# One-pass logits with doubled queries and keys, an earlier memory attention, filler at four rates, and a regrouped opening and output projection in a two-layer encoder trunk

## The chip, the cores and the metric

The kernel runs on one core of one Trainium2 chip. The metric is the device time of one execution in microseconds (us). Three runs of the kernel before gave 1203.88, 1205.63 and 1206.22; their median, 1205.63, is the time before.

## The reference, cut to what matters

The trunk has two layers on 512 tokens of width 1024 in fp32. Each layer normalises the tokens, projects them, mixes them over the sequence, attends beside that to 256 memory tokens in four heads, projects the concatenated result, adds it to the residual, and then runs a gated MLP with a causal convolution. Layer 0 mixes by differential attention in six heads of two 64-wide halves; layer 1 mixes by chunked gated linear attention (GLA).

```python
# layer 0, per head h, half m (0, 1), query block of 128 tokens
q = rms_norm(q, qk_norm_g[0]) * (d ** -0.5)          # d = 64
k = rms_norm(k, qk_norm_g[1])
logits = einsum('bhmqd,bhmkd->bhmqk', q, k) + bias   # keys up to the query's chunk
p = softmax(logits)
w = p[:, :, 0] - lam * p[:, :, 1]
o = rms_norm(w @ v, out_norm_g) * (1.0 - lam_init)
# both layers
x = x + concat([mix, cross]) @ w_out[i]
x = x + conv_ffn(rms_norm(x, ffn_norm[i]))
```

## The kernel before, in words

**Precision and weights.** Large products are made from float32r operands in one pass each. An operand is split into a hi part (a cast) and a lo part (what the cast lost), and three matmuls, hi·hi, hi·lo and lo·hi, stand for one fp32 matmul: gemm (L250 to L252) for projections whose output has tokens on the partitions, product (L267 to L269) for those whose output is transposed. The moving side is up to 512 columns wide. Weights come in pieces: SP loads a raw tile, ACT casts hi (L200), DVE subtracts lo (L201); activations are split by ACT (L233) and DVE (L234). Small products, the attention's logits (L613), values (L649) and all transposes (L169), are plain fp32 matmuls; the profile shows an fp32 matmul that is no transpose as two records.

**Order.** The order on PE is the order of the text. On the other engines a scheduler orders the instructions. Between steps of the attention PE gets filler: a queue of units of large products (class Filler, L89) from which `fill(us)` takes as many as its argument pays for, by costs written in the code. `need` runs the queue up to a mark, `flush` runs all of it.

**Memory of the matmuls.** There are four tags of PSUM banks with two banks each: mm for large products, sm for values and some large products, lg for logits, tp for transposes.

**Layer 0's attention** (diff_layer, L554) is a loop of 28 steps t (L681). Step t does logits(t), values(t - 2), a fill, turn(t - 1), a slot of memory attention, and a fill again; a step index u is head u // 4, query block i = u % 4, and the logits of block i have 128·(i + 1) keys. prepare(h) (L581) transposes the four token blocks of a head's normalised q and of its k into a tp bank each, and ACT copies them out (L589). The two 64-wide halves of a head then lie on partitions 0 to 63 and 64 to 127, and logits (L613) multiplies each half by itself, in 64-row matmuls, into its own lg bank; from the second block on each is cut in two. DVE adds the bias and takes the maximum (L618), ACT takes the exponentials (L621), DVE joins the halves. turn (L631) transposes the weights, values (L641) multiplies them by v, finish(h) (L658) transposes the head's output and splits it. Heads 0 and 1 are prepared before the loop, the others at t = 7, 8, 15, 16; their norms (group_norm, L299: squares on ACT L303, sums L304 and the scaling L307 on DVE) are at t = 5, 6, 13, 14. Memory attention (MemAttn, L473) starts its slots at t = M0 = 12, with its norm at t = 8, the memory keys' transposes (keys0) at t = 9 and its queries (L487) at t = 11. Each step fills twice 3.0 us up to t = 13 and 1.2 us from there.

**The output projection** (out_proj) goes in parts given by PASS, a list per layer of output column groups c with the mix tiles ks that they take; mix tiles 0 to 5 are the heads and 6, 7 the memory attention. A part's tiles are filler; the last part of each layer comes behind the loop. A finished tile is added to the residual on DVE (update, L969), split for the MLP (L233, L234), and its squares are summed (L335). The MLP starts with row_scales (L1026), which needs the squares of all tiles.

**The opening** (L354 to L420) loads, on SP, the columns of norm gains (cols_a), then the x tiles and weight blocks in turn, and multiplies the first projection as they arrive, in an order written by hand on all engines (operands(k), matmuls L420); ACT's queue loads the first weights. Its four banks are then evicted with r_x, the tokens' norm factors.

**GLA** makes its gates (L799 to L807) for four heads, each a small matmul (L800) into an lg bank, then ACT (absolute value, exponential, logarithm: L802 to L804) and DVE (L805, a scan L807).

Of the kernel before, what the change touches and what calls it, by code (L numbers as in the profile page):

```python
# [10 lines left out]
F32 = mybir.dt.float32  # L11
F32R = mybir.dt.float32r
# [19 lines left out]
WB = 5  # L32
FA, FB = 3.0, 1.2
K8 = tuple(range(KT))
# [3 lines left out]
         [(2, (6, 7, 4, 5)), (0, (4, 5)), (3, (6, 7, 4, 5)), (1, (4, 5))]],  # L38
        [[(c, (0, 1, 2, 6, 7)) for c in C4], [(c, (3, 4, 5)) for c in C4]])

# [87 lines left out]
@with_exitstack  # L128
def trunk(ctx, tc, x_t, mem_t, wpack, cols_a_d, cols_d, conv_d, gate_d, rel_bias, diff_lambda, consts, onehot, out):
    nc = tc.nc  # L130
# [167 lines left out]

    def group_norm(pool, y, nb, ng, d, on_dve=False):  # L299
        ss = small("ss")  # L300
        for b in range(0, nb, 2):
            sq = xtile()[:, :2 * ng * d]
            A.activation(sq, y[:, b:b + 2].rearrange("p b n -> p (b n)"), AF.Square)  # L303
            V.reduce_sum(ss[:, b * ng:(b + 2) * ng], sq.rearrange("p (g d) -> p g d", d=d), axis=AX.X)  # L304
        r = rsqrt(ss[:, :nb * ng], nb * ng, 1.0 / d, on_dve)
        yv = y.rearrange("p b (g d) -> p (b g) d", d=d)
        V.tensor_mul(yv, yv, r.unsqueeze(2).to_broadcast([128, nb * ng, d]))  # L307

# [35 lines left out]
    def small_vectors():  # L344
        for c in (c_dq, c_mq(0), c_mq(1)):
            V.tensor_scalar_mul(c, c, 0.125)
        V.tensor_scalar_mul(c_do, c_do, 1.0 - LAM_INIT)
        for t in range(3):
            V.tensor_scalar_mul(c_go(t), c_go(t), 0.5)
        lam(lv, xtile()[:, 0:128].rearrange("p (a b) -> p a b", a=2))  # L350
# [3 lines left out]
    with tc.tile_pool(name="ini", bufs=1) as ip, tc.manual_schedule(engines={E.Activation, E.DVE, E.Pool, E.SP}):  # L354
# [12 lines left out]
        A.dma_start(raws[0][:, blk(0, S)], wpack[0, :, blk(0, S)])  # L367
        load(cols_a, cols_a_d)
        for k in range(KT):
            xT[k] = xtile()  # L370
            load(xT[k], x_t[k])
            if k:
                load(raws[k // 2][:, blk(k % 2, S)], wpack[k // 2, :, blk(k % 2, S)])
        at[0] = 4
# [9 lines left out]
        def operands(k):  # L384
            if k % 2 == 0:
                split_w[0] = [wp.tile([128, WTILE], F32R, name=n, tag=n, bufs=WB) for n in ("whi", "wlo")]
            c = blk(k % 2, S)
            hi, lo = split_w[0]
            xh[k], xl[k] = split_tiles()
            if k == 0:  # L390
                V.tensor_copy(hi[:, c], raws[0][:, c])
                V.tensor_sub(lo[:, c], raws[0][:, c], hi[:, c].bitcast(F32))
                split(xh[0], xl[0], xT[0], c_attn(0, 0))
            else:
                split(xh[k], xl[k], xT[k], c_attn(0, k))
                split_weights(c, raws[k // 2], hi, lo)
            parts.append((hi[:, c], lo[:, c]))
            squares(xT[k], acc)
# [41 lines left out]
    def mem_kv(l):  # L440
# [18 lines left out]
        def keys():  # L459
            F.need(f"kv{l}")  # L460
            p = bank("lg")
            for hp in range(2):
# [4 lines left out]
             (lambda: token_rsqrt("lg", mem_acc[0], 2, r_mem)) if l == 0 else None)  # L467
        F.add(0.0, lambda: group_norm(None, km[0], 2, 4, 64))
        F.mark(f"kv{l}")
# [3 lines left out]
    class MemAttn:  # L473
# [4 lines left out]
        def norm(self):  # L478
            group_norm(self.pool, self.qm, NB, 4, 64, self.on_dve)

# [72 lines left out]

    def diff_layer(pool, mix):  # L554
        r = r_x[:, 0]
# [7 lines left out]
        def halves(d0, d1):  # L563
# [3 lines left out]
            return ev  # L567

        def project_qk(pr):
            qk[pr] = (pool.tile([128, NB, 256], F32, name="qs", bufs=1),  # L570
                      pool.tile([128, NB, 256], F32, name="ks", bufs=1))
            gemm(xh, xl, NB, ("qk", pr), 512, halves(*qk[pr]))
            F.mark(f"qk{pr}")

        heads = {}

        def norms(pr, i):
            F.need(f"qk{pr}")
            group_norm(pool, qk[pr][i], NB, 4, 64)

        def prepare(h):  # L581
            pr, j = divmod(h, 2)
            t2 = []
            for src, g, nm in zip(qk[pr], (c_dq, c_dk), ("qT", "kT")):
                dst = pool.tile([128, S], F32, name=nm, bufs=3)
                p = bank("tp")
                for b in range(NB):
                    transpose(p[:, blk(b)], src[:, b, blk(j)])
                A.activation(dst, p, AF.Copy, scale=g)  # L589
                t2.append(dst)  # L590
            sm = cp.tile([128, 16], F32, name="smd", tag="smd")
            heads[h] = dict(q=t2[0], k=t2[1], s2=sm.rearrange("p (m b) -> p m b", b=8),
                            nm=small("nmd"), rc=small("rcd"), v=vs[pr], j=j)

        live = {}

        def logits(u):
# [10 lines left out]
            pls = bank("lg"), bank("lg")  # L608
            cuts = (0, nk) if i == 0 else (0, nk // 2, nk)
            for k0, k1 in zip(cuts, cuts[1:]):  # L610
                for m in range(2):
                    hh = blk(m, 64)
                    mm(pls[m][:, k0:k1], H["q"][hh, blk(i)], H["k"][hh, k0:k1], start=True, stop=True)  # L613
            for m in range(2):
# [26 lines left out]
        def values(u):  # L641
            h, i = divmod(u, 4)
            H = heads[h]
            if i == 0:
                F.need(f"v{h // 2}")
                H["po"] = bank("sm")
            po, wT = H["po"], live.pop(u)
            for kb in range(i + 1):
                mm(po[:, blk(i)], wT[:, blk(kb)], H["v"][:, kb, blk(H["j"])], start=kb == 0, stop=kb == i)  # L649
            if i == 3:  # L650
                rs = small("rs0")
                V.reciprocal(rs[:, :NB], H["s2"][:, 0, :NB])
                o = H["o"] = pool.tile([128, NB, 128], F32, name="o", bufs=2)
                V.tensor_mul(o, po.rearrange("p (b d) -> p b d", d=128),
                             rs[:, :NB].unsqueeze(2).to_broadcast([128, NB, 128]))
                group_norm(pool, o, NB, 1, 128)

        def finish(h):  # L658
            p = bank("tp")
            for b in range(NB):  # L660
# [4 lines left out]

        qk[0] = (pool.tile([128, NB, 256], F32, name="qs", bufs=1),
                 pool.tile([128, NB, 256], F32, name="ks", bufs=1))
        ev = halves(*qk[0])
        for b in range(NB):
# [4 lines left out]
        F.mark("v0")  # L674
        F.fill(10.0)
        prepare(0)
        F.fill(1.2)
        prepare(1)
        ma = MemAttn(pool, 0, qm, mix, False)
        M0 = 12  # L680
        for t in range(28):  # L681
            if t == 0:
# [6 lines left out]
                ops1, keys1 = mem_kv(1)  # L689
            if t == 8:  # L690
                ma.norm()
            if t == 9:
                keys0()
# [9 lines left out]
            if t in (20, 24):  # L703
                out_proj(0, mix, t // 4 - 4, None)
            f = FA if t < 14 else FB
            if t == 11:
                ma.queries()
# [5 lines left out]
            if t in (5, 6, 13, 14):  # L713
                norms((t + 3) // 8, (t + 3) % 8)
            if 0 <= t - 1 < 24:
                turn(t - 1)
            ma.slot(t - M0)
            F.fill(f)
            if t in (7, 8, 15, 16):
                prepare(2 * (t // 7) + (t + 1) % 8)  # L720
            if t % 4 == 3 and t >= 7:
                finish(t // 4 - 1)
        F.flush()


    def gla_layer(pool, mix, acc):
# [71 lines left out]
        for h in range(4):  # L798
            pz = bank("lg")  # L799
            mm(pz[:96], gw3[:, blk(h, 96)], gl3, start=True, stop=True)  # L800
# [133 lines left out]
        for h in range(4):  # L934
# [15 lines left out]
            outputs(h, 1)  # L950
            group_norm(pool, o_[h], NB, 1, 192, True)
            F.fill(f)
# [29 lines left out]

    def out_proj(l, mix, part, acc):
        got = {}
        turns = cycle(("mm", "sm") if part == len(PASS[l]) - 1 else ("mm",))

        def unit(c, ks, n, i):
            if i == 0:
                if c not in got:
                    got[c] = weights(("o", l, part, c))  # L990
                got["p"] = bank(next(turns))
            p = got["p"]
            product(p, got[c], n, [mix[k] for k in ks], (i,))
            if i == len(ks) - 1:
                update(2 * c + n, p, None if acc is None else (lambda k: c_ffn(l, k)), acc, G if l else V)
        todo, kk = tiles(l, part)
        for n in todo:
            for i in range(len(kk[n // 2])):
                F.add(0.65, lambda n=n, i=i: unit(n // 2, kk[n // 2], n % 2, i))

# [71 lines left out]
    for l in range(2):  # L1072
        with tc.tile_pool(name=f"at{l}", bufs=2) as pool:
            mix = [None] * 8
            if l == 0:
                diff_layer(pool, mix)
            else:
                gla_layer(pool, mix, acc)
            acc = [None]
            out_proj(l, mix, len(PASS[l]) - 1, acc)  # L1080
            F.flush()
        with tc.tile_pool(name=f"ff{l}", bufs=2) as pool:
# [74 lines left out]
```

## Time and profile before

| | us |
|---|---|
| median of three runs | 1205.63 |
| profiled execution | 1205.31 |
| its span | 1203.5 |
| PE busy | 1188.3 (99%) |
| DVE busy | 759.8 (63%) |
| ACT busy | 540.7 (45%) |
| POOL busy | 23.5 (2%) |

All times of the trace are from one profiled execution; it took 1205.31 us, of which 1203.5 are the span from the first instruction to the last. The costliest groups of PE are the one-pass matmuls of 512 columns, L267 to L269 in mm banks alone 460 of each line. The chip's DMA queues moved 117.80 MB, most of it weights, at a mean of 98 GB/s. Stages that the text speaks of, by the trace's clock: the opening up to about 31 us, the loop of layer 0's attention from the first logits at 45.35 to the last at 227.78, its end up to L1026 at 269.30, GLA's gates around 650, the end of layer 1's mixer at 842.64.

In the views of the trace a line gives start, duration, engine, line of the code, operation, result <- operands, the shape, and, in brackets, how long the engine was idle before it and what released it. "x8" joins eight neighbours of one kind.

### The profile page before, as it was taken

To read this page: it belongs to the slowest core of one execution; us is meant where nothing else is said; L and a number is where in the kernel's file an instruction comes from. 1 tells how busy PE (TensorE), PEld (TensorE's weight loads), DVE (VectorE), ACT (ScalarE), POOL (GpSimd) and SP (SyncE) were. 2 spreads that over 40 slices of the span, in tenths; PEclk is the share of its full clock that TensorE was granted. 3 is DMA by queue.
4 is the path that set the end of the run, shared out by engine and by line. 5 is a ranking of instruction groups with operands and counts; after the bars stand their busy time and mean duration, and the time that the engine had idled before them with its cause. 6 is when DMAs were issued, how large, how long until landed. Compare 5 with 4: busy or idle time off the path is not lost.

```text
span 1203.5 us, 14757 instructions
## 1 busy us (share of the span) xinstructions
PE 1188.3 (99%) x5672; PEld 975.0 (81%) x5672; DVE 759.8 (63%) x1259; ACT 540.7 (45%) x915; POOL 23.5 (2%) x37
## 2 busy tenths in 40 slices
PE   9999999999999999999999999999999999999998
PEld 6887777778888888888787888987888888888887
DVE  7566578887776534767546446768677653476741
ACT  6666666554444222434436444536444432243420
POOL 0000000000000000000020000003000000000000
PEclk9999999999999999999999999999999999999999
DMA  8432231232332331422342221234233233232231
GB/s 275 132 101 84 80 118 49 71 105 88 98 112 70 123 105 53 130 80 88 116 146 74 70 71 57 62 127 133 78 98 112 71 123 97 67 122 84 87 114 44
DMA packets 39413, 117.80 MB, mean 98 GB/s; under 512 B 4688, under 2 KB 5769, under 8 KB 39343
## 3 DMA queue, kind: packets, MB, share of 16 engines
q1 hardware_dynamic: 39198, 116.60, 30.5%
q8 instruction: 44, 0.72, 0.2%
q10 hardware_dynamic: 144, 0.26, 0.1%
q14 instruction: 27, 0.21, 0.1%
HBM read 112.63 MB, written 4.21 MB: 97 GB/s over the span
## 4 chain that ended last, share of the span: by engine, by line
PE 90%; DVE 5%; ACT 3%; issue 1%; DMA 1%; SPq 0%; DVEq 0%; ACTq 0%
PE ps_mm L268 8%; PE ps_mm L269 8%; PE ps_mm L267 8%; PE ps_sm L267 6%; PE ps_sm L268 6%; PE ps_sm L269 6%; PE ps_mm L250 6%; PE ps_mm L252 6%; PE ps_mm L251 5%; PE ps_tp L267 3%; PE ps_tp L268 3%; PE ps_tp L269 3%; PE ps_lg L268 3%; PE ps_lg L269 3%; PE ps_lg L267 3%; PE ps_tp L169 2%
## 5 line engine op out<-in xcount | busy, mean ns | idle before, releaser
L200 ACT CAST whi<-raw 128x1024 fp32r<-128x1024 f32 (+2 forms) x214 | 207.7, 976 | 247.5 <-PE ps_tp L268 133.8
L201 DVE TENSOR_TENSOR wlo<-raw,whi 128x1024 fp32r<-128x1024 f32 (+2 forms) x214 | 240.8, 1136 | 111.0 <-ACT whi L200 109.9
L267 PE MATMUL ps_mm<-xsh,whi 128*128 128x512 f32 x460 | 182.5, 397 | 0.2 <-DVE xt L969 0.2
L268 PE MATMUL ps_mm<-xsl,whi 128*128 128x512 f32 x460 | 179.4, 390 | 1.4 <-DVE xsl L234 1.3
L269 PE MATMUL ps_mm<-xsh,wlo 128*128 128x512 f32 x460 | 179.3, 390 | 0.0
L268 PE MATMUL ps_sm<-xsl,whi 128*128 128x512 f32 x372 | 144.7, 389 | 0.0
L267 PE MATMUL ps_sm<-xsh,whi 128*128 128x512 f32 x372 | 144.7, 389 | 0.0
L269 PE MATMUL ps_sm<-xsh,wlo 128*128 128x512 f32 x372 | 144.7, 389 | 0.0
L250 PE MATMUL ps_mm<-whi,xsh 128*128 128x512 f32 (+2 forms) x352 | 138.2, 393 | 0.1
L252 PE MATMUL ps_mm<-whi,xsl 128*128 128x512 f32 (+2 forms) x352 | 131.4, 373 | 0.3 <-DVE xsl L234 0.3
L251 PE MATMUL ps_mm<-wlo,xsh 128*128 128x512 f32 (+2 forms) x352 | 130.6, 371 | 0.0
L1019 ACT ACTIVATE cvo<-u,cv 128x512 f32<-128x512 f32 x88 | 71.6, 815 | 114.0 <-DVE u L1017 113.6
L268 PEld LDWEIGHTS ps_mm<-xsl,whi 128*128 128x128 f32 x460 | 86.5, 188 | 20.2 <-DVE xsl L234 2.7
L267 PEld LDWEIGHTS ps_mm<-xsh,whi 128*128 128x128 f32 x460 | 86.4, 188 | 18.2 <-DVE xt L969 0.9
L269 PEld LDWEIGHTS ps_mm<-xsh,wlo 128*128 128x128 f32 x460 | 86.3, 188 | 18.1
L1020 DVE SCALAR_TENSOR_TENSOR cvo<-u,cv,cvo 128x512 f32<-128x512 f32 x88 | 65.9, 749 | 31.6 <-ACT cvo L1019 31.4
L268 PEld LDWEIGHTS ps_sm<-xsl,whi 128*128 128x128 f32 x372 | 69.8, 188 | 14.6
L269 PEld LDWEIGHTS ps_sm<-xsh,wlo 128*128 128x128 f32 x372 | 69.8, 188 | 14.5
L267 PEld LDWEIGHTS ps_sm<-xsh,whi 128*128 128x128 f32 x372 | 69.8, 188 | 14.4
L252 PEld LDWEIGHTS ps_mm<-whi,xsl 128*128 128x128 f32 x352 | 66.1, 188 | 12.7 <-DVE xsl L234 0.5
L250 PEld LDWEIGHTS ps_mm<-whi,xsh 128*128 128x128 f32 x352 | 66.3, 188 | 10.7 <-issue 0.9
L251 PEld LDWEIGHTS ps_mm<-wlo,xsh 128*128 128x128 f32 x352 | 66.5, 189 | 9.5
(247 smaller groups left out, 1767.9 us busy)
## 6 DMA issues: line engine op xcount, KB each, us to landing
raw<-in_wpack_dram SPq DMA_DIRECT2D x176, 512.0 KB, 3.5
raw<-in_wpack_dram SPq DMA_DIRECT2D x27, 256.0 KB, 3.5
xt<-in_x_t_dram SPq DMA_DIRECT2D x16, 256.0 KB, 5.3
xres<-xt SPq DMA_DIRECT2D x8, 256.0 KB, 3.5
xt<-xres SPq DMA_DIRECT2D x8, 256.0 KB, 4.4
out_dram<-xt SPq DMA_DIRECT2D x8, 256.0 KB, 2.0
bt<-bias_d SPq DMA_DIRECT2D x6, 256.0 KB, 5.2
raw<-in_wpack_dram SPq DMA_DIRECT2D x4, 384.0 KB, 2.9
```

The source lines that it names most:

```text
L169: nc.tensor.transpose(dst, src, ident[:n, :n])
L200: A.copy(hi[:, c], raw[:, c])
L201: V.tensor_sub(lo[:, c], raw[:, c], hi[:, c].bitcast(F32))
L250: mm(p, sh[k][:, blk(b)], hi, start=k == 0, stop=False)
L251: mm(p, sh[k][:, blk(b)], lo, start=False, stop=False)
L252: mm(p, sl[k][:, blk(b)], hi, start=False, stop=k == KT - 1)
L267: mm(p, hi[:, blk(n)], bh, start=i == first, stop=False)
L268: mm(p, hi[:, blk(n)], bl, start=False, stop=False)
L269: mm(p, lo[:, blk(n)], bh, start=False, stop=i == last)
L1019: A.activation(c, u[:, 2:], AF.Identity, scale=cv[l][:, 2, j:j + 1], bias=cv[l][:, 3, j:j + 1])
L1020: V.scalar_tensor_tensor(c, u[:, 1:S + 1], cv[l][:, 1, j:j + 1], c, op0=ALU.mult, op1=ALU.add)
```

## The change

1. q and k of a head pair lie in tiles of twice the width, [128, 4 blocks, 4 halves, 2, 64]. For q, slot 1 gets hi (ACT copy to float32r) and slot 0 the rest (DVE); for k the second slot is a copy (ACT). prepare takes one half m of a head: four transposes of a q half, four of a k half, an ACT copy of q (now hi and lo stacked on 128 rows), a split of k (ACT and DVE). Logits are, per half, two one-pass matmuls on 128 rows, with k's hi and lo, over all keys at once. The gains of q and k are joined in the k columns.
2. Memory attention moves from M0 = 12 to 8, its norm to t = 5, keys0 and the queries to t = 7.
3. The fills are 3.2 us (t < 8), 2.1 (t < 13), 1.5 (t < 20) and 1.3, instead of 3.0 (t < 14) and 1.2; ahead of the loop 12.5 instead of 10.0, and 1.2 behind each of four half prepares.
4. In the steps with a prepare, its first half comes behind the first fill, ahead of turn, and the second behind the second fill.
5. Of layer 0's last part of the output projection, four units (twelve matmuls) that do not take head 5 are queued at t = 26 and flushed ahead of finish(5); the rest comes behind the loop. Banks of last parts go mm, mm, sm, sm instead of mm, sm.
6. In the opening the gain columns and x tile 0 are one tensor, loaded first in two parts, and split in two halves; the separate load of cols_a goes behind the last weights.
7. The matmuls of GLA's gates use lg and sm banks in turn.
8. In layer 1, column group 3 takes mix tiles 6 and 7 in the last part instead of the first.

```diff
-FA, FB = 3.0, 1.2
+STEPS, FILL = (8, 13, 20), (3.2, 2.1, 1.5, 1.3)
...
-        [[(c, (0, 1, 2, 6, 7)) for c in C4], [(c, (3, 4, 5)) for c in C4]])
+        [[(c, (0, 1, 2, 6, 7)) for c in (0, 1, 2)] + [(3, (0, 1, 2))],
+         [(c, (3, 4, 5)) for c in (0, 1, 2)] + [(3, (6, 7, 3, 4, 5))]])
...
+        V.tensor_mul(c_dk, c_dk, c_dq)
...
-        load(cols_a, cols_a_d)
-        for k in range(KT):
+        head = ip.tile([128, 32 + S], F32, name="head")
+        for c in (slice(0, 32 + S // 2), slice(32 + S // 2, 32 + S)):
+            load(head[:, c], head_d[:, c])
+        xT[0] = head[:, 32:]
+        for k in range(1, KT):
...
-                split(xh[0], xl[0], xT[0], c_attn(0, 0))
+                for t in (blk(0, S // 2), blk(1, S // 2)):
+                    split(xh[0][:, t], xl[0][:, t], xT[0][:, t], col(0, head))
...
         def norms(pr, i):
             F.need(f"qk{pr}")
-            group_norm(pool, qk[pr][i], NB, 4, 64)
+            y = qk[pr][i].rearrange("p b g t d -> p (b g) t d")
+            group_norm(y[:, :, 0], 64)
+            if i:
+                A.copy(y[:, :, 1], y[:, :, 0])
+            else:
+                A.copy(y[:, :, 1].bitcast(F32R), y[:, :, 0])
+                V.tensor_sub(y[:, :, 0], y[:, :, 0], y[:, :, 1])
-        def prepare(h):
+        def prepare(h, m):
...
+            q, k = (t[:, :, 2 * j + m].rearrange("p b t d -> p b (t d)") for t in qk[pr])
+            p = bank("tp")
+            for b in range(NB):
+                transpose(p[:, blk(b)], q[:, b])
+            H["q", m] = pool.tile([128, S], F32R, name=f"qT{m}", bufs=2)
+            A.copy(H["q", m], p)
+            p = bank("tp")
+            for b in range(NB):
+                transpose(p[:, blk(b)], k[:, b])
...
+            split(H["kh", m], H["kl", m], p, c_dk)
...
-            cuts = (0, nk) if i == 0 else (0, nk // 2, nk)
-            for k0, k1 in zip(cuts, cuts[1:]):
-                for m in range(2):
-                    hh = blk(m, 64)
-                    mm(pls[m][:, k0:k1], H["q"][hh, blk(i)], H["k"][hh, k0:k1], start=True, stop=True)
+            for m in range(2):
+                for part in ("kh", "kl"):
+                    mm(pls[m][:, :nk], H["q", m][:, blk(i)], H[part, m][:, :nk], start=part == "kh",
+                       stop=part == "kl")
...
-        F.fill(10.0)
-        prepare(0)
-        F.fill(1.2)
-        prepare(1)
+        F.fill(12.5)
+        for h in range(2):
+            for m in range(2):
+                prepare(h, m)
+                F.fill(1.2)
...
-        M0 = 12
+        M0 = 8
...
-            if t == 8:
+            if t == 5:
                 ma.norm()
-            if t == 9:
+            if t == 7:
                 keys0()
...
+            if t == 26:
+                rest = out_proj(0, mix, 3, acc, 5)
+            f = FILL[bisect(STEPS, t)]
-            if t == 11:
+            if t == 7:
                 ma.queries()
...
+            ahead = 2 * (t // 7) + (t + 1) % 8 if t in (7, 8, 15, 16) else None
+            if ahead:
+                prepare(ahead, 0)
             if 0 <= t - 1 < 24:
                 turn(t - 1)
             ma.slot(t - M0)
             F.fill(f)
-            if t in (7, 8, 15, 16):
-                prepare(2 * (t // 7) + (t + 1) % 8)
+            if ahead:
+                prepare(ahead, 1)
+            if t == 27:
+                F.flush()
             if t % 4 == 3 and t >= 7:
                 finish(t // 4 - 1)
+        rest()
...
-            pz = bank("lg")
+            pz = bank(("lg", "sm")[h % 2])
...
-        turns = cycle(("mm", "sm") if part == len(PASS[l]) - 1 else ("mm",))
+        turns = cycle(("mm", "mm", "sm", "sm") if part == len(PASS[l]) - 1 else ("mm",))
...
+        units = [(n, i) for n in todo for i in range(len(kk[n // 2]))]
+        first = [(n, i) for n, i in units if n in todo[:2] and kk[n // 2][i] != late] if late is not None else []
+        units = first + [u for u in units if u not in first]
```

## The prediction

> **What bounds the kernel now.** I read the page's busy times first, then the chain that ended last, then the timeline of PE, group by group, through the stages that the change touches. From the page:
>
> ```profile
> PE 1188.3 (99%) x5672; PEld 975.0 (81%) x5672; DVE 759.8 (63%) x1259; ACT 540.7 (45%) x915; POOL 23.5 (2%) x37
> PE 90%; DVE 5%; ACT 3%; issue 1%; DMA 1%; SPq 0%; DVEq 0%; ACTq 0%
> ```
>
> The chain runs through PE nearly everywhere, and the granted clock is 1.00 throughout. So the time is PE's instructions, priced from one start to the next (an instruction's own duration overlaps its neighbours'), plus the places where PE waits. PE's order is the order of the text; I compared both kernels' orders and give each difference a price. The timeline of PE has the prices (start, duration, instruction, and in brackets the idle time before it and what ended it):
>
> ```profile
> 52.79 0.71 PE L613 MATMUL ps_lg<-kT,qT 64*128 64x128 f32 x8
> 53.44 0.50 PE L250 MATMUL ps_mm<-whi,xsh 128*128 128x512 f32 x1
> ...
> 227.45 0.40 PE L269 MATMUL ps_mm<-xsh,wlo 128*128 128x512 f32 x1
> 227.78 1.14 PE L613 MATMUL ps_lg<-kT,qT 64*128 64x256 f32 x8
> 228.84 0.71 PE L649 MATMUL ps_sm<-v,xt 128*128 128x128 f32 x4
> ```
>
> ```profile
> 781.42 0.29 PE L252 MATMUL ps_mm<-whi,xsl 128*128 128x256 f32 x1
> 781.54 0.28 PE L250 MATMUL ps_mm<-whi,xsh 128*128 128x256 f32 x1
> ```
>
> Filler of 512 columns starts every 0.2275 us (53.78 to 58.95 is such a run), 256 columns every 0.12. The widest logits group takes 1.06 (227.78 to 228.84), the others 0.64 to 0.65 (52.79), 0.85 (59.27) and 0.42 (110.76). A logits group that follows filler starts about 0.1 late (227.45 to 227.78 is 0.33, not 0.2275), and so does the first filler behind fp32 matmuls. Four transposes take 0.43 (108.80 to 109.23), 0.109 each.
>
> The waits that the change touches:
>
> ```profile
> 108.80 0.60 PE L169 MATMUL ps_tp<-C,qs 128*128 128x128 f32 x4
> 109.23 0.60 PE L169 MATMUL ps_tp<-C,ks 128*128 128x128 f32 x4
> 110.18 0.66 PE L169 MATMUL ps_tp<-C,o 128*128 128x128 f32 x4 [0.34 <-ACT qT L589]
> ...
> 190.87 0.66 PE L169 MATMUL ps_tp<-C,ks 128*128 128x128 f32 x4 [1.08 <-DVE xt L513]
> ...
> 650.52 0.47 PE L800 MATMUL ps_lg<-xsh,xsl 96*96 96x512 f32 x1 [0.92 <-DVE xt L805]
> 658.28 1.28 PE L496 MATMUL ps_lg<-kmT,xt 64*128 64x256 f32 x8
> 841.95 0.50 PE L268 MATMUL ps_mm<-xsl,whi 128*128 128x512 f32 x1 [1.18 <-DVE xsl L234]
> ```
>
> There are two tp banks, so a third group of transposes waits for a copy to free one: from 109.23 to 110.18 is 0.95, where 0.43 would do.
>
> **The change, part by part.** *Logits.* A head has steps i = 0 to 3. Before: 0.42 + 0.64 + 0.85 + 1.06 = 2.97, six heads 17.8, and 0.1 at 16 places behind filler, 1.6: 19.4. After: four one-pass matmuls of 128, 256, 384 and 512 columns. The last three have rows (0.12; 0.174 on the line between 256 and 512; 0.2275): 0.48, 0.70, 0.91. One of 128 columns has none. Its bounds are the transpose of the same shape, 0.109, and a 128-column fp32 matmul of L649 (two records, 0.224). I take 0.109, since 256 columns already cost 0.12: 0.44. A head 2.53, six 15.2: **-4.2** (-1.5 with the upper bound).
>
> The Trainium skill ("TensorE: Matmul & The Clock Gate", Part 3, row/col tiling) says that matmuls on distinct 64-row groups run concurrently, the pair spanning one matmul and a few ns. That speaks against this change: the old halves would already be paired, each 128 columns at about 0.21 (L649's single one takes 0.224), a head 2.1, and the logits would go from 12.6 to 15.2. The trace disagrees: its widest group takes 1.06, where that gives 0.84, so the measurement decides.
>
> *Preparation.* Each head has 16 transposes instead of 8: 48 x 0.109 = **+5.2**; and two more runs that break the filler, **+0.2**. ACT gets per head two more evictions of 512 columns, DVE two subtractions like L234 (0.67); per pair ACT two copies of 1024 columns and DVE one subtraction like L201 (1.15). DVE: 12 x 0.67 + 3 x 1.15 = 11.5 us more. Where this falls, DVE is nearly full already (busy PE, PEld, DVE, ACT, POOL; clock; DMA):
>
> ```profile
> 160.00:240.00 80.00, 77.04 (x481) 61.85 (x480) 67.28 (x179) 47.15 (x134) 0.15 (x1) 1.00 0.27 88
> ```
>
> *Waits in the loop.* Between the first logits (45.35) and the last (227.78) PE takes 182.4, where the unstalled prices sum to 174.6, so waits are 7.8: 5.3 at logits for an lg bank (the largest 1.2, behind keys0 at 120 and at 172 to 175), 2.5 around prepares (0.55 at 109, 0.6 at 182, 1.24 at 189). After: the two halves of a prepare stand apart, and a group of transposes follows each half on the tp banks. I count four turns behind first halves at 0.55, two finishes at 0.55, two logits that wait for the new k-lo at 0.5, and 0.6 for the rest: 4.9. The finer filler and memory attention four steps earlier, away from the steps where DVE is full, lower the lg waits to some 2.0; where filler is thinned to 1.3 and DVE has the doubles' subtraction (steps 13 and 14: DVE 15.9, PE 13.5) 0.7 comes back. Sum 7.6, **-0.2**. Ends: all hidden, -6; each wait a cast longer, +4.5. The moved memory attention issues no DMA; the filler's weight loads on SP keep their order.
>
> *End of layer 0's attention.* Before, from the transposes of head 5 (246.21) to L1026 (269.30) is 23.1: 96 matmuls (21.8), and 1.2 of transposes and waits. Ten matmuls stand between the transposes and the first that needs head 5's lo (249.20, an L268), so the split is covered. DVE runs almost without a gap:
>
> ```profile
> 249.96 0.69 DVE L969 TENSOR_TENSOR xt<-xt,ps_mm 128x512 f32<-128x512 f32 x1 [0.82 <-PE ps_mm L269]
> ...
> 268.57 0.68 DVE L335 TENSOR_TENSOR xt<-xt 128x512 f32<-128x512 f32 x1
> ```
>
> Twelve matmuls (2.7) go ahead of the transposes, and the next ones need head 5: they wait for ACT's hi (0.69) and DVE's lo (0.75), uncovered now. PE alone would need 84 x 0.2275 + 0.4 + 1.4 + 0.2 = 21.1. DVE needs 8 adds (0.60), 8 splits (0.67), 7 squares (0.60) and 4 casts' lo parts (1.15), 19.0 from the first add, which comes some 3 after the transposes: 22.0. The work behind is 1.1 shorter and that ahead 2.7 longer: with 0.3 for bank waits between, **+1.9**; if PE alone set it +0.7, with one cast more +2.8.
>
> *Opening.* The first x tile and its columns come first in two halves, so the first matmul (5.38, after ACT's xsh) starts about 1 earlier. But the banks of the next product come free only by ACT's evictions from 29.63, which wait for r_x on a DVE chain that stays, and PE arrives at 31.23, 1.6 later; 0.8 of that is needed for the first evictions. **-0.7** (-1.0 to 0).
>
> *GLA gates.* The waits 0.92 and 0.33 go with the second bank tag. But the logits at 658.28 wait for ACT: the gates' logarithms, a table load (656.25), L487 (657.54). PE gets there earlier and waits longer: **0** (-1.3 if ACT too moves up).
>
> *Last output tiles of layer 1.* Six-matmul runs give way to eight transposes in a row (a tp wait of 0.75), and the last wait of 1.2 gets twelve matmuls more behind the transposes: **-0.7** (-1.3 to +0.3).
>
> Sum: -4.2 + 5.2 + 0.2 - 0.2 + 1.9 - 0.7 + 0 - 0.7 = +1.5. On the profiled execution's 1205.31 (span 1203.5 and 1.8 around it) this is **1206.8**. The median of the three runs is 0.3 above that execution, they spread over 2.3, and a measurement can tell about 0.2%, 2.4 us.
>
> **The rivals.** *A, slower: casts in front of the tp copies.* ACT and DVE serve in their order. A copy that frees a tp bank, or the k-lo that logits need, can land behind a weight cast (0.98 on ACT, 1.14 on DVE). 190.87 shows it: 1.08 spent waiting for DVE. The change doubles the places. If half of the eight waits grow by a cast, +4.5: **1211.3**. It decides where ACT and DVE have a cast ready at the moment of the transposes, as they do with DVE at 84% from 160 to 240. For it: this row; against: at 109, with the same engines loaded, 0.55 was all.
> *B, slower: 128 columns cost like L649* (24 x 0.115 = 2.7): **1209.5**. Against: the 256-column row at 0.12.
> *C, faster: the finer order hides the waits.* With memory attention early and filler between the halves, the prepares' waits drop to the two finishes and keys0's lg wait goes (-3.8 in the loop), and the first adds come early enough at the end to leave PE as the bound (-1.2): **1201.8**. For it: of 182 us only 7.8 are waits, most at few steps that the change rearranges, and ACT is 41% idle there; against: DVE gets 11.5 more.
> *D: the logits don't get cheaper* is the concurrency above; the rows exclude it but for 0.02.
>
> **How the numbers follow.** Forecast 0.36 (own range 1203.6 to 1208.0, within 0.2%), A 0.22, B and D 0.08, C 0.34. Faster by over 0.2% is C, 0.34; slower A, B and D, 0.30; within 0.36. Cases of both signs hold most of the chance, so the range takes both: 1199.5 (C with the opening's and gates' lower ends) to 1211.8 (A).
>
> **What would show it.** Logits groups of 0.44 to 0.91 and 48 more transposes at 0.109; tp waits of about 0.5 behind each half, not over 1 (A) nor absent (C); DVE without gaps from the first add to L1026, and that stretch near 22; the first matmul near 4.4 but the bank wait at 30 longer; the logits of layer 1's memory attention still at their place. Wrong if ACT's or DVE's order puts casts ahead of the copies, or if filler runs out before a finish.

## The result, and the profile after

The changed kernel takes 1214.41 us (median of 4 runs, 1213.63 to 1215.17) against 1205.65 for the kernel before; the ratio is 1.0075 with a 95% interval of 1.0063 to 1.0088. It is 8.8 us slower; I had forecast 1206.8, with 1211.8 as the upper end. Five places on PE cut both profiles into stages (us); the two profiled executions differ by 9.6:

| stage | before | after | difference | forecast |
|---|---|---|---|---|
| opening, to the next product's first matmul | 31.23 | 31.43 | +0.2 | -0.7 |
| loop, to head 5's transposes | 214.97 | 223.74 | +8.8 | +3.7 |
| those to L1026 (now L1076) | 23.10 | 23.05 | -0.05 | -0.8 |
| MLP, to layer 1's memory attention | 388.98 | 388.97 | 0 | 0 |
| that to the second L1026 | 184.36 | 185.22 | +0.9 | -0.7 |
| rest of the span | 360.9 | 360.7 | -0.2 | 0 |

The twelve matmuls of output tiles that now stand ahead of head 5's transposes move 2.7 from the end into the loop; the forecast column has them too. Against the forecast the loop lost 5 us, layer 1's stretch 1.6, the opening 0.9 and the end 0.8. From the profile's page after, the busy times and the chain that ended last:

```profile
PE 1189.3 (98%) x5648; PEld 982.9 (81%) x5648; DVE 770.2 (63%) x1278; ACT 554.2 (46%) x936; POOL 23.0 (2%) x37
PE 88%; DVE 6%; ACT 4%; issue 1%; DMA 1%; SPq 0%; DVEq 0%; ACTq 0%
```

PE is busy hardly longer, but two percent of the chain have gone from PE to DVE and ACT. PE's timeline shows where (L645 are the logits, L171 transposes, L506 the memory attention's logits, L252 to L254 filler):

```profile
177.25 1.00 PE L535 MATMUL ps_sm<-vm,xt 128*128 128x64 f32 x8
182.38 2.55 PE L506 MATMUL ps_lg<-kmT,xt 64*128 64x256 f32 x8 [4.13 <-DVE nmd L651]
184.86 1.12 PE L171 MATMUL ps_tp<-C,xt 128*128 128x128 f32 x4
185.63 0.78 PE L252 MATMUL ps_mm<-whi,xsh 128*128 128x512 f32 x1
186.21 0.63 PE L253 MATMUL ps_mm<-wlo,xsh 128*128 128x512 f32 x1
186.63 0.53 PE L254 MATMUL ps_mm<-whi,xsl 128*128 128x512 f32 x1
187.00 0.39 PE L252 MATMUL ps_mm<-whi,xsh 128*128 128x512 f32 x1
...
192.60 0.55 PE L171 MATMUL ps_tp<-C,xt 128*128 128x128 f32 x3 [1.11 <-ACT qT L621]
...
197.01 0.66 PE L171 MATMUL ps_tp<-C,o 128*128 128x128 f32 x4 [0.32 <-ACT qT L621]
...
198.38 0.33 PE L645 MATMUL ps_lg<-kl,qT 128*128 128x128 f32 x1 [0.43 <-DVE kl L236]
```

A wait of 4.13 us, for an lg bank, is longer than any other of either profile. And what stands behind it runs slowly. The profile before has the same instructions at a like place without a wait:

```profile
171.38 1.13 PE L496 MATMUL ps_lg<-kmT,xt 64*128 64x256 f32 x8
172.44 0.66 PE L169 MATMUL ps_tp<-C,xt 128*128 128x128 f32 x4
172.85 0.47 PE L250 MATMUL ps_mm<-whi,xsh 128*128 128x512 f32 x1
```

From start to start, the eight matmuls take 2.48 (before 1.06), the transposes 0.77 (0.41), three fillers 1.37 (0.78), together 2.4 too much, up to 187.00. The windows say why (length; busy PE, PEld, DVE, ACT, POOL; granted clock):

```profile
170.00:180.00 10.00, 8.25 (x50) 6.85 (x48) 9.45 (x27) 6.30 (x18) 0.00 (x0) 1.00 0.76 248
180.00:186.50 6.50, 4.12 (x14) 3.24 (x15) 5.50 (x14) 4.17 (x12) 0.00 (x0) 0.51 0.27 104
187.00:190.00 3.00, 3.00 (x17) 2.44 (x16) 3.00 (x8) 2.11 (x7) 0.00 (x0) 1.00 0.00 0
```

The clock is halved for 6.8 us (180.09 to 186.91), from the middle of the wait on. What DVE does in that wait:

```profile
177.28 0.68 DVE L309 TENSOR_TENSOR o<-o,rs_y 128x512 f32<-128x512 f32 x1
...
178.29 1.23 DVE L309 TENSOR_TENSOR qs<-qs,rs_y 128x1024 f32<-128x1024 f32 x1
180.62 1.23 DVE L605 TENSOR_TENSOR qs<-qs 128x1024 f32<-128x1024 f32 x1 [1.11 <-ACT qs L604]
181.77 0.55 DVE L651 CUSTOM_DVE_ANT_0 xt<-ps_lg,bt 128x384 f32<-128x384 f32 x1
```

The logits of step 14 were ready at about 175.3. Their bias add (L651), which frees the lg banks, stands on DVE behind the third pair's q norm, and that now includes a wait for ACT's cast and the subtraction L605. Three terms of the sum against the new trace: the logits groups take 0.40, 0.47, 0.71 and 0.91 where nothing holds them up (14.9 for six heads, forecast 15.2); a transpose takes 0.109; the waits around prepares come to 5.7 (forecast 4.9).

The end, and the start of layer 1's memory attention, in the same view:

```profile
276.57 0.49 PE L269 MATMUL ps_mm<-xsh,whi 128*128 128x512 f32 x1 [0.77 <-ACT xsh L235]
277.62 0.50 PE L270 MATMUL ps_mm<-xsl,whi 128*128 128x512 f32 x1 [0.55 <-DVE xsl L236]
...
667.19 1.43 PE L506 MATMUL ps_lg<-kmT,xt 64*128 64x256 f32 x8 [1.78 <-ACT xt L497]
```

### The profile page after: what moved, and what is told of

It is laid out like the page before. It is cut to its first block, busy times and chain, and to the rows that moved or that the text cites. A ratio compares the mean times of both kernels' runs of the same rounds, so it can differ in the third digit from the quotient of the medians.

```text
span 1213.1 us, 14747 instructions
## 1 busy us (share of the span) xinstructions
PE 1189.3 (98%) x5648; PEld 982.9 (81%) x5648; DVE 770.2 (63%) x1278; ACT 554.2 (46%) x936; POOL 23.0 (2%) x37
## 4 chain that ended last, share of the span: by engine, by line
PE 88%; DVE 6%; ACT 4%; issue 1%; DMA 1%; SPq 0%; DVEq 0%; ACTq 0%
PE ps_mm L270 8%; PE ps_mm L271 8%; PE ps_mm L269 8%; PE ps_sm L270 7%; PE ps_sm L269 7%; PE ps_sm L271 7%; PE ps_mm L252 5%; PE ps_mm L254 5%; PE ps_mm L253 5%; PE ps_tp L269 3%; PE ps_tp L270 3%; PE ps_tp L271 3%; PE ps_lg L270 3%; PE ps_lg L271 3%; PE ps_lg L269 3%; PE ps_tp L171 2%
## 5 line engine op out<-in xcount | busy, mean ns | idle before, releaser
L269 PE MATMUL ps_mm<-xsh,whi 128*128 128x512 f32 x452 | 179.3, 397 | 2.1 <-ACT xsh L235 1.5
L270 PE MATMUL ps_mm<-xsl,whi 128*128 128x512 f32 x452 | 176.4, 390 | 0.8 <-DVE xsl L236 0.8
L271 PE MATMUL ps_mm<-xsh,wlo 128*128 128x512 f32 x452 | 176.2, 390 | 0.0
L271 PE MATMUL ps_sm<-xsh,wlo 128*128 128x512 f32 x380 | 147.8, 389 | 0.0
L270 PE MATMUL ps_sm<-xsl,whi 128*128 128x512 f32 x380 | 147.8, 389 | 0.0
L269 PE MATMUL ps_sm<-xsh,whi 128*128 128x512 f32 x380 | 147.8, 389 | 0.0
L252 PE MATMUL ps_mm<-whi,xsh 128*128 128x512 f32 (+2 forms) x352 | 139.3, 396 | 0.3 <-ACT ks L586 0.2
L254 PE MATMUL ps_mm<-whi,xsl 128*128 128x512 f32 (+2 forms) x352 | 132.0, 375 | 0.3 <-DVE xsl L236 0.3
L1070 DVE SCALAR_TENSOR_TENSOR cvo<-u,cv,cvo 128x512 f32<-128x512 f32 x88 | 65.9, 749 | 31.6 <-ACT cvo L1069 31.4
L269 PEld LDWEIGHTS ps_sm<-xsh,whi 128*128 128x128 f32 x380 | 71.3, 188 | 14.9
L254 PEld LDWEIGHTS ps_mm<-whi,xsl 128*128 128x128 f32 x352 | 66.6, 189 | 12.9 <-DVE xsl L236 0.5
L252 PEld LDWEIGHTS ps_mm<-whi,xsh 128*128 128x128 f32 x352 | 67.0, 190 | 11.1 <-issue 0.8
```

Of the source, the lines that this page charges most:

```text
L252: mm(p, sh[k][:, blk(b)], hi, start=k == 0, stop=False)
L254: mm(p, sl[k][:, blk(b)], hi, start=False, stop=k == KT - 1)
L269: mm(p, hi[:, blk(n)], bh, start=i == first, stop=False)
L270: mm(p, hi[:, blk(n)], bl, start=False, stop=False)
L271: mm(p, lo[:, blk(n)], bh, start=False, stop=i == last)
L1070: V.scalar_tensor_tensor(c, u[:, 1:S + 1], cv[l][:, 1, j:j + 1], c, op0=ALU.mult, op1=ALU.add)
```

## The experiments

**Theory 1**: the loop's loss is DVE's (and ACT's) chain for the third pair's q, which stands in front of the bias add, and the halved clock behind the wait. **Theory 2**: the earlier memory attention makes the wait. The number that opens each result is the run's time in us. Times are medians; "before" was 1205.2 to 1205.6 in each set.

**e1**, the subtraction on POOL.

```diff
-                V.tensor_sub(y[:, :, 0], y[:, :, 0], y[:, :, 1])
+                (G if pr == 2 else V).tensor_sub(y[:, :, 0], y[:, :, 0], y[:, :, 1])
```

> The changed kernel, but the subtraction that makes q's lo part for the third head pair runs on POOL instead of DVE. Theory 1: the wait of 4.13 us at the memory attention's logits (182.38) is DVE's chain for the norm of that pair: the scaling of qs, 1.1 us of waiting for ACT's cast, 1.15 us of subtraction, and only then the bias add that frees the lg banks. Then the wait falls by about 2.3 to 1.8 us, the clock stays at 1.00 behind it (another 2.2 us), and the time is about 1210. Theory 2, the memory attention's earlier place makes the wait whatever DVE does there: it stays near 4 and the time near 1214. If POOL's subtraction is slow enough to delay the transposes of q, up to 1 us comes back there.

1211.13. PE's and DVE's timelines:

```profile
179.29 2.28 PE L506 MATMUL ps_lg<-kmT,xt 64*128 64x256 f32 x8 [1.80 <-DVE nmd L651]
```

```profile
177.53 1.23 DVE L309 TENSOR_TENSOR qs<-qs,rs_y 128x1024 f32<-128x1024 f32 x1
178.68 0.55 DVE L651 CUSTOM_DVE_ANT_0 xt<-ps_lg,bt 128x384 f32<-128x384 f32 x1
```

The bias add follows the scaling at once and the wait is 1.80, as theory 1 had it. The clock was halved all the same, for 3.4 us: 1.8 us of waiting suffice. The time fits the forecast of about 1210 partly by luck. In the profiles the loop is only 1.3 shorter than with the change (222.5 against 223.7); the rest of the gain is layer 1's stretch, where the clock stayed up (183.7 against 185.2), and a shorter opening (30.6 against 31.4).

**e2**, memory attention at the old steps (M0 = 12, norm, keys and queries at 8, 9, 11).

> The changed kernel with memory attention, its norm, keys and queries back at the steps of the kernel before (first slot at 12). The even steps still hold a pair of lg banks each for the memory attention, step 14 among them. Theory 1 (the q norm's chain on DVE): the wait at step 14 stays at 3 to 4 us with the clock drop behind it, time 1213 to 1216. Theory 2 (the earlier memory attention): the wait goes to below 1 and the time falls by 5 to 6 us to 1208 to 1209.

1215.38, and the wait is there, 4.11, with the clock down behind it. Theory 2 falls.

**e3**, memory attention from step 9 (M0 = 9).

> The changed kernel with the memory attention's first slot at 9 instead of 8, so that its logits fall on steps 9, 11, 13, 15 and step 14 has none. Theory 1: PE then meets the held lg banks only at the logits of step 15, about 2 us of work later, so the wait is 1.5 to 2.5 us instead of 4.13, the clock drop shrinks or goes, and the time is 1210 to 1212.5. Theory 2: no different from 1214, since memory attention is still early.

1217.94: missed. PE now waits at two places, 1.30 at the logits of step 14, for a bank that ACT's exponentials of the memory attention (L513) free, and 3.22 at the transposes of k, for the copy that doubles k:

```profile
191.94 1.12 PE L171 MATMUL ps_tp<-C,ks 128*128 128x128 f32 x4 [3.22 <-ACT ks L602]
```

The clock was halved at both (3.4 and 6.8 us). So the long wait isn't bound to the memory attention's banks: PE meets the chain of the doubled q and k elsewhere.

**e4**, four dummy matmuls ahead of the wait.

```diff
+            if self.l == 0 and b == 3:
+                p = bank("tp")
+                for _ in range(4):
+                    mm(p, ident, C[:, 0:512], start=True, stop=True)
```

> The changed kernel with four dummy fp32 matmuls of 512 columns (about 3.4 us, result read by nobody) put in front of the memory attention's logits that wait 4.13 us. They add no data that anything needs. If the slow matmuls behind the wait (granted clock 0.66 from 180 to 190) come from PE's idleness, the wait shrinks to some 0.7 us of idle time, the eight matmuls behind it take 1.06 instead of 2.48 us, and the time is 2.2 us shorter, 1212.2. If the slowness has another cause it stays, and the time is unchanged at 1214.4 or longer.

1211.94, 2.5 less with more work on PE:

```profile
176.72 3.65 PE L505 MATMUL ps_tp<-C 128*128 128x512 f32 x8
181.02 1.61 PE L510 MATMUL ps_lg<-kmT,xt 64*128 64x256 f32 x8 [0.65 <-DVE nmd L655]
182.56 0.66 PE L171 MATMUL ps_tp<-C,xt 128*128 128x128 f32 x4
```

The clock is 1.00 there, and the eight matmuls take 1.54, so the slowness came from PE's idleness. The shorter time is not from this place, though. A later wait (1.60, for k's copy) halved the clock once, and the loop takes 224.2 in this profile, 0.5 more than with the change; what is shorter is layer 1's stretch, where the clock stayed up (183.6 against 185.2), and the opening (30.2 against 31.4).

**e5**, fills of 3.0 at steps 13 and 14; **e9**, the third pair's norms at steps 12 and 13.

```diff
+            f = 3.0 if t in (13, 14) else FILL[bisect(STEPS, t)]
```

```diff
+            if t in (5, 6, 12, 13):
+                norms(*((1, t - 5) if t < 8 else (2, t - 12)))
```

> The changed kernel with fills of 3.0 us at steps 13 and 14 instead of 1.5; the eight units are taken from the flush at the end of the loop and the steps before it. Theory 1, as it stands after e1 to e4: from the norm of the third pair (step 13) to its transposes (step 15) DVE and ACT need longer than the work that PE has there, and PE meets the difference somewhere (at the memory attention's logits, or at the transposes of k), with the clock halved behind it. Then 5.5 us of matmuls moved in front remove the 4.13 us wait and the clock drop, and later steps give back up to 2 us: 1208 to 1210. If the wait comes from the DVE order alone, which more filler would push back as well, it stays and the time is 1213 to 1216.

> The changed kernel with the norms of the third head pair at steps 12 and 13 instead of 13 and 14, so that the chain of norm, cast and subtraction has a step more before the transposes of step 15, and the bias adds that stand behind q's chain on DVE are those of the odd step 13, where memory attention wants no lg bank. Theory 1: no wait over 1.5 us between 160 and 195, the clock stays at 1.00, and the time is 1208 to 1210. If the loss is in the amount of DVE's work and not in its place, the wait moves elsewhere and the time stays at 1213 to 1217.

1217.38 and 1213.66: both missed. The wait shrinks (1.64 and 1.99), but filler spent there is missing later. In step 19, from its logits to the next, the change has 15 matmuls of filler, e5 none and e9 six; e5 then waits 1.43 and 2.65 at later transposes and 1.09 at logits, e9 1.46 at 223.51, and in both the clock fell again between 250 and 270. The filler of the loop is used up by its end; moving it, or the norms (whose `need` draws filler forward: 48 matmuls instead of 24 in step 12 of e9), moves the waits.

**e6**, the kernel before with the new logits and prepares alone; **e7**, with the new fills and memory attention alone.

> The kernel before with the one-pass logits alone: doubled q and k, prepares in halves and placed as in the change; memory attention, fills, opening, gates and output tiles as before. PE's own work rises by about 1 us (logits 14.9 instead of 19.4, transposes 5.2 more), the transposes' bank waits by 2 to 3. Step 13 still fills 3.0, so theory 1 leaves a wait of 0 to 2 us at the q norm: 1208 to 1211. If the thin filler is the whole cause of the loss, the time is 1205 to 1207.

> The kernel before with the change's fills (3.2, 2.1, 1.5, 1.3; 12.5 ahead of the loop) and memory attention from step 8 alone; fp32 logits and prepares as before. Without the doubling DVE's chain at steps 13 and 14 is 2.3 us shorter (no cast to wait for, no subtraction). Theory 1: a wait of 1 to 2.5 us is left at the memory attention's logits, with or without a clock drop: 1206 to 1209. If the doubling is the whole cause, no wait over 1 us and 1203 to 1206.

e6 1216.59: 11 us slower than the kernel before, more than expected, with waits of 1.62 and 3.54 for ACT's copy of k:

```profile
190.14 0.55 PE L169 MATMUL ps_tp<-C,ks 128*128 128x128 f32 x3 [3.54 <-ACT ks L595]
```

e7 1203.16, ratio 0.9981 (0.9972 to 0.9990): the schedule is a gain of 2.4 for the old logits. Its PE passes step 14 without any wait:

```profile
173.04 0.92 PE L614 MATMUL ps_lg<-kT,qT 64*128 64x192 f32 x8
...
175.82 1.00 PE L526 MATMUL ps_sm<-vm,xt 128*128 128x64 f32 x8
176.75 1.30 PE L497 MATMUL ps_lg<-kmT,xt 64*128 64x256 f32 x8
```

So the new fills and the earlier memory attention don't make the loss by themselves, and e6 has it with the new logits and the old fills: most of it comes with the new logits. It doesn't follow that the filler has no part in it: in step 13 the changed kernel has less of it than e7, for all that the two have the same fills (see e13 to e15).

**e8**, the output tiles not regrouped; **e10**, the gates on lg alone.

```diff
-                rest = out_proj(0, mix, 3, acc, 5)
...
-        rest()
         F.flush()
+        out_proj(0, mix, 3, acc)
+        F.flush()
```

> The changed kernel with the last part of layer 0's output projection wholly behind the loop, as before (its banks still in the new turn). From head 5's transposes to L1026's matmul the change has 23.05 us with 84 matmuls, the kernel before 23.1 with 96. If DVE's chain sets that stretch, the twelve matmuls fit into it again: the stretch stays at 23.1 and the loop is 2.7 us shorter, 1211.7. If the twelve matmuls are paid wherever they stand, the stretch grows to 25 and the time stays at 1214.

> The changed kernel with the gates' matmuls of layer 1 on lg banks alone, as before. In the profile after, PE waits 1.93 us in one piece for the first logits of layer 1's memory attention (667.19), and the clock falls behind it; in e1 to e4 the same wait left the clock at 1.00, and the stretch from there to the second L1026 took 183.6 instead of 185.2. If it is the joined wait that trips the clock in some executions, the old banks, which spread it over three places, give 183.6 in every profile, and the time is 0 to 1.6 us shorter: 1212.8 to 1214.4. If the second tag gains anything, the time is up to 1.2 longer.

e8 1211.91: from head 5's transposes to L1026, 96 matmuls fit into 22.75 us where the change needs 23.05 for 84. e10 1212.22, a little under the expected 1212.8, and layer 1's stretch is 183.67. The second tag joins PE's waits before layer 1's memory attention into one of 1.8 to 2.2 us; behind it the clock fell in 5 of the 11 profiles with the new gates (stretch 185.1 to 185.2) and not in the other 6 (183.6 to 183.7), never in e10 and e11, where the waits stay 0.9 and 0.3. Where the clock fell, the stretch is some 1.5 longer.

**e11**, the edits of e8, e9 and e10 together.

> The changed kernel with three edits: the norms as in e9, the gates as in e10, the output tiles as in e8. Sum of what these should give (5.0, 0.8, 2.5): 1206. It tells whether the one-pass logits break even once their chain has room; the transposes' bank waits (5.7 us in the profile after, 1.6 in e7) stay.

1214.01: missed by 8. The early norms draw the filler forward, and without the twelve matmuls too little is left before head 5's transposes: 36 matmuls from the last logits on, where e8 has 45. PE waits there 3.45 for DVE's norm.

**e13 to e15**, with parts of the new logits left out (second slots zero; no lo of k; both).

```diff
-            if i:
-                A.copy(y[:, :, 1], y[:, :, 0])
-            else:
-                A.copy(y[:, :, 1].bitcast(F32R), y[:, :, 0])
-                V.tensor_sub(y[:, :, 0], y[:, :, 0], y[:, :, 1])
+            G.memset(y[:, :, 1], 0.0)
```

```diff
-            split(H["kh", m], H["kl", m], p, c_dk)
+            A.activation(H["kh", m], p, AF.Copy, scale=c_dk)
```

> The changed kernel without the doubling's work on ACT and DVE: q's cast and subtraction and k's copy are left out, and the second slots are zeros written by POOL (so q's lo parts are missing from the logits). Transposes, splits of k and all matmuls stay. e9 and e5 showed that a step more of lead or six us more of filler only move the wait, so the question is which added work makes it. If it is the doubling (per pair 2 us of ACT and 1.15 of DVE, in a chain between the norm and the transposes): no wait over 1.5 us and no clock drop at 160 to 200, 1207 to 1209. If it is the prepares' evictions and bank waits, the time stays above 1212.

> The changed kernel without k's lo parts: the subtraction on DVE (12 times 0.67 us) is left out and the second matmul of each logits pair takes k's hi again (so the logits are wrong by that). Doubling, transposes and the count of matmuls stay. If the doubling makes the large wait: only the two logits' waits for k's lo (0.6 each) and perhaps 1 us of DVE's lag go, 1211.5 to 1213.5. If DVE's subtractions behind the transposes make it, the wait at 182 falls below 2 and the time is 1207 to 1210.

> The changed kernel without both (e13 and e14 together): what stays of the new logits is 48 more transposes, two ACT evictions more a head, and the cheaper matmuls. If the loss lies in the doubling and the splits, the loop is then near that of e7 plus its twelve more matmuls and the bank waits (212.8 + 2.7 + 2 to 4), and the time 1205.5 to 1208. If the transposes and bank waits are the loss, 1210 or more.

1210.62, 1211.61 and 1208.29: neither alone comes as low as the expectation for the guilty one. The wait at the memory attention is 4.13 in e14, and in e13:

```profile
178.52 1.61 PE L506 MATMUL ps_lg<-kmT,xt 64*128 64x256 f32 x8 [1.79 <-DVE nmd L647]
```

So the doubling makes 2.3 us of the wait, and 1.8 remain even without it or k's lo (1.81 in e15). DVE's bias add and the work between the logits of steps 13 and 14, in e7 and then in e13:

```profile
175.84 0.55 DVE L619 CUSTOM_DVE_ANT_0 xt<-ps_lg,bt 128x384 f32<-128x384 f32 x1
161.68:173.04 11.36, 11.36 (x66) 9.45 (x65) 9.08 (x22) 8.91 (x22) 0.00 (x0) 1.00 0.18 59
...
177.91 0.55 DVE L647 CUSTOM_DVE_ANT_0 xt<-ps_lg,bt 128x384 f32<-128x384 f32 x1
166.03:172.94 6.91, 6.91 (x45) 6.10 (x43) 6.35 (x15) 5.43 (x13) 0.00 (x0) 1.00 0.30 100
```

In e7 the bias add starts 0.9 before PE comes to the memory attention's logits (176.75), in e13 1.2 behind that point (176.73). From the logits of step 14 to there PE takes about as long in both, 3.71 and 3.79. What differs is the step before, 11.36 against 6.91. There e7 has 36 matmuls of filler, and e13, like the change, 18. Between opening and loop e7 had run 66 such matmuls and the change 84, since it fills behind each of four half prepares; `need` in step 13 of e7 runs 18 more than in e13. Meanwhile ACT works off its queue: it turns to the last tile of the third pair's projection at 170.36 in e7, 2.7 before the logits of step 14, and in e13 at 171.54, only 1.4 before them. That this is where the last 1.8 us come from is a reading of the traces; no run changes the filler ahead of the loop alone.

Against e7 the change's 11.2 us divide, as far as medians add up, into 6.1 for doubling and splits together (e15), 2.5 for the regrouping (e8), and 2.6 for what is left of the new logits, with the gates and the last tiles. The medians hold the falls of the clock in layer 1, which come by chance. By the loop and its end alone, in the profiles, it is 5.5, 2.1 and 3.6.

**e12 and e16**, the kernel before with the new fills and memory attention, and layer 1's last tiles regrouped; e16 has the new opening as well.

> The kernel before with the change's fills and memory attention (as e7, 1203.2) and the last output tiles of layer 1 regrouped as in the change, nothing else. The stretch from layer 1's memory attention to its L1026 should fall from 184.4 to 183.6 as in e1 to e4: 1202.4. If the regrouping gains nothing without the other parts, 1203.2.

> The kernel of e12 (1202.05) with the change's opening: first x tile and gain columns as one tensor in two halves, cols_a behind the weights. I forecast 0.7 us for the opening (0 to 1.0). In the profiles so far the opening's end (first matmul of the next product) lies at 31.1 to 32.1 in four kernels with the old opening and at 30.2 to 32.5 in ten with the new, means 31.55 and 31.32, so 0.2 would be 1201.8; and from 0.6 on it would show.

1202.05 and 1201.47; the ratio to the kernel before is 0.9971 for both (0.9961 to 0.9982 and 0.9960 to 0.9983). Both beat both kernels of the case. Against each other, they show no gain of the opening: the difference lies within the noise.

## Why the prediction was wrong, by its steps

- **Logits, transposes, breaks** (-4.2, +5.2, +0.2): right, by the prices above (-4.5, +5.2, and no late start behind filler any more).
- **Waits in the loop** (-0.2): this step failed. It held a term of 0.7 for DVE's lag at steps 13 and 14, from DVE's 15.9 us of work against PE's 13.5; why 0.7 of this difference of 2.4 it did not say. It measured 6.5: 4.1 of waiting and 2.4 at half clock. I had counted DVE's work as a sum over two steps, and not asked what stands in front of the bias add at the moment when PE needs its bank. There the wait for ACT's cast counts too (1.11 of DVE idle), and what DVE was already behind. The other waits, 5.7 at prepares and 2.0 at logits, were near the 4.9 and 2.0 of the sum.
- **The clock** stood in no term, since it was 1.00 throughout the profile before. No wait there is over 1.2 us, once the opening has begun. After the change it costs 2.4 in the loop and some 1.5 in layer 1's stretch.
- **End of layer 0's attention** (+1.9): the mechanism was right, the split uncovered and DVE's chain the bound; e8 gives 2.5 by the medians, 2.1 by the stages. PE's last waits, 0.77 and 0.55, are for ACT's and DVE's split of the last tile.
- **Opening** (-0.7): not to be seen. The first matmul starts at 4.90 instead of 5.38 (about 4.4 was expected), but e16 against e12 has the same ratio, and the stage ends at 30.2 to 32.5 from one profile to the next.
- **Gates** (0): right in its first order, the wait only moves. It costs some 1.5 where the joined wait trips the clock, as in the profile after.
- **Last tiles of layer 1** (-0.7): right; 183.65 against 184.36 where the clock stays up, 183.84 with the old logits (e12, e16).
- **Rival A** forecast slower, by casts in front of the copies that free tp banks. Those waits came out 0.8 above my count in all, with one of 1.11, so it was not that; its thought, an engine's queue ahead of what frees a bank, belonged to lg and the bias add. **B** falls by the rows (0.1125 for 128 columns). **C** was right in part for the schedule alone (e7's loop takes 212.8 against 215.0, a gain of 2.2 where C has 3.8) and wrong for the logits beside it.
- **The range's ends** were added up wrongly: C's 1201.8 less 0.3 for the opening and 1.3 for the gates is 1200.2, not 1199.5, and A's sum is 1211.3, not 1211.8. Neither bears on the outcome.

That the doubling, the splits and the regrouping make most of the loss is shown. Where the last 1.8 us of waiting in e13 and e15 come from is not; the 18 matmuls of filler that step 13 lacks are the likely cause.

## What to carry to other kernels

Where one engine is 99% busy, price what the others do at the moment at which it needs a buffer back: go through the queue of the engine that frees the buffer, latencies of its partners included, and not through sums over a stage. A cheaper form of one step that adds a chain of cast, subtract and copy on other engines can lose many times what it saves. Filler is a fixed stock: more of it at one wait, or ahead of a loop, is a wait further on. And compare experiments stage by stage: two of them here (e1, e4) got much of their gain from a stage that their edit did not touch.

## What the runs showed of the hardware

The granted clock of PE halves after waits, in pieces of some 3.4 us. Waits of 3.2 to 4.15 us cost 3.4 to 6.8 us at half clock in seven profiles; one of 2.65 (e5) and one of 3.45 (e11) cost nothing. Waits of 1.60 to 1.99 in the loop halved it for 3.4 us in six profiles (e1, e4, e5, e9, e11, e15) and not in e13 (1.79) nor at e6's 1.62; short ones in a row did (1.30 and 0.29 in e3; 0.74, 0.78 and 0.29 around 255 in e9, which made its end 1.6 longer, 24.65 instead of 23.05); single waits up to 1.2, and those of 1.43 to 1.48 (e5, e6, e9, e11), never did. The same wait of 1.8 at layer 1's memory attention did so in 5 of 11.

More than the length of a wait, its place tells. In each profile the changes of the clock lie whole multiples of 3.41 us apart (after: 180.09, 186.91, 668.19, 671.61). If each trace is cut at these points into stretches of that length, and PE's idle time is added up in each, the clock never fell behind a stretch with 1.47 us or less, and it fell behind 21 of the 26 with 1.55 or more (counting those that began at full clock, in 18 profiles). The waits of 1.79 and 2.65 that cost nothing lie across a border (0.46 and 1.33; 1.32 and 1.46); the 3.45 of e11 (1.89 and 1.55) stays unexplained. The borders fall differently in each execution: the other three runs of e13 had a mean granted clock of 0.997, the profiled one 1.00, and took 0.8 to 2.1 us longer than that one.

The Trainium skill ("TensorE: Matmul & The Clock Gate", Part 1) tells of a free-running window of about 3.4 us by which the clock is gated to half, and has it fall after at least one idle window. The lengths of 3.4 and 6.8 us and the role of the place agree with the window; the idle time does not, since about 1.6 us of it in a window were enough here, and the measurement decides.

A subtraction of 1024 columns took 2.36 us on POOL and 1.23 on DVE.
